# Output projections with the last two head blocks held back and four outputs begun early, in a hybrid attention encoder on one Trainium2 core

## The chip, the core and the metric

The kernel runs on one core of a Trainium2 chip. The metric is device time in microseconds (us). Five engines work in parallel, each through its own queue in order: PE (matrix products), DVE (VectorE, elementwise), ACT (ScalarE, activations and copies), POOL (GpSimd, elementwise) and SP (which issues the transfers). They meet only in semaphores.

## The reference

512 tokens of width 1024 go through two residual mixer layers, each followed by a SwiGLU feed-forward block, in float32. Layer 0 mixes by latent attention and dilated windows, layer 1 by grouped-query attention. What matters here is the end of each mixer and the start of its feed-forward block:

```python
x = x + heads @ w_out                      # heads: 6 (layer 0) or 8 (layer 1) blocks of 128 columns
n = x * rsqrt(mean(x * x) + 1e-6) * gain   # RMS norm over the 1024 columns
f = silu(n @ w_gate) * (n @ w_up)          # hidden width 2816 = 22 blocks of 128
x = x + f @ w_down
```

## The kernel before

Everything is held transposed: x is eight tiles d8 to d15 of 128 columns by 512 tokens. A float32 number is split into a high part (float32r) and a remainder, and a product is three matmuls (lines L165 to L167: high by high, high by low, low by high). A weight load (`load`) is a transfer, a high copy on ACT (L154) and a subtraction on POOL (L155). A scheduler fixes each engine's order when the program is built, so what the source writes is not always the order on the engine.

**Mixer's end.** `mix_part` projects the head blocks that are ready early, one output tile after the other, and adds each to x (L645, DVE); its matmuls fill the gaps between the attention's steps. The last block comes from the last attention head: its weighted sum (pv) goes through ACT and DVE (L363, L366, L368) before PE may use it. `mix_last` then projects the late blocks for all eight outputs n, one after the other, each in a PSUM bank of the tag `acc`, of which there are two. After the add (L655) `nr.feed` makes the next layer's input parts of tile n: high on ACT (L207), low on DVE (L208, reads two SBUF tiles), and a square on ACT (L198), summed on POOL (L202).

**Start of the feed-forward block.** Gate and up products (`og`, `ou`) of hidden blocks f0 and f1 start from those parts before the norm is known. The norm's column sums are eight one-column matmuls (L220), then DVE (L223), POOL's power (L225), and four matmuls that spread it (L232). The products of f1 beyond the first three blocks are written behind the spread. After it DVE makes the scaled inputs (L692, L693) and their sums for a seven-product scheme (`sums`: L671 to L683; the last low parts of each pair are L683) and the results of f0 to f3 (L863 to L866). In `Seven` a unit adds weight tiles into the sums `tab` and `bias` and splits each into high (ACT, L180) and low (DVE, L181). The products named b11, b21, t1 to t4, b22 are matmuls of 256 columns (L742).

Of the kernel before, what the change touches and what calls it, by code (L numbers as in the profile page):

```python
# [9 lines left out]
F32 = mybir.dt.float32  # L10
F32R = mybir.dt.float32r
AF = mybir.ActivationFunctionType
ALU = mybir.AluOpType
AX = mybir.AxisListType

P = 128
# [9 lines left out]
FIRST = 4  # L26
# [5 lines left out]
QTAGS = ("pt", "pt", "acc")  # L32
WARM = 14
HP, NHP = 100, 200
QFIRST = 3
GOUT = {6: (0, 3), 12: (3, 6)}
FILL = [1] * 12 + [2] * 4
# [56 lines left out]
def encoder_kernel(ctx: ExitStack, tc: tile.TileContext, a, out):  # L94
    nc = tc.nc
# [7 lines left out]
    def psum(tag):  # L103
        return ps.tile([P, 512], F32, tag=tag, bufs=BANKS[tag], name=f"ps_{tag}")
# [5 lines left out]
    def E(dt=F32):  # L110
        return U("e", dt, bufs=4)
# [32 lines left out]
    def load(views, k, low=None):  # L144
        raw = U("wraw", bufs=2, shape=(P, WCOLS))
        hi = U("whi", F32R, bufs=3, shape=(P, WCOLS))
        lo = U("wlo", F32R, bufs=3, shape=(P, WCOLS))
        n = 0
        for v in views:
            a, b = v.shape[1], v.shape[2]  # L150
            nc.sync.dma_start(raw[:, n:n + a * b].rearrange("p (a b) -> p a b", a=a), v)
            n += a * b
        r, h, l = raw[:, :n], hi[:, :n], lo[:, :n]
        nc.scalar.copy(h, r)  # L154
        (low or nc.gpsimd).tensor_sub(l, r, h.bitcast(F32))  # L155
        if k is None:
            return h, l
        return h.rearrange("p (k n) -> p k n", k=k), l.rearrange("p (k n) -> p k n", k=k)

    def wview(w, k0, k1, n0, n1):  # L160
        return w[k0 * P:k1 * P, n0:n1].rearrange("(k p) n -> p k n", p=P)

    def mm3(dst, lhs, rhs, first, last):

        nc.tensor.matmul(dst, lhsT=lhs[0], rhs=rhs[0], start=first, stop=False)  # L165
        nc.tensor.matmul(dst, lhsT=lhs[0], rhs=rhs[1], start=False, stop=False)  # L166
        nc.tensor.matmul(dst, lhsT=lhs[1], rhs=rhs[0], start=False, stop=last)  # L167
# [15 lines left out]
    class Norm:  # L183


        def __init__(self, dst=None):
            self.dst = dst
            self.parts = []
            self.acc = U("nacc", bufs=2)
            self.sums = [self.acc]  # L190
            self.n = 0
# [83 lines left out]
    for k in range(KB):  # L275
# [4 lines left out]
        xt = E()  # L280
# [126 lines left out]
    for k in range(3):  # L407
        o = proj(wblock(k * P), xs, QTAGS[k])
# [29 lines left out]
    hd0 = Heads([(f"d{b}", f"d{4 + b}") for b in range(4)] + [("d16", "d17"), ("d18", "d19")])  # L438


    for sp in range(2):
# [9 lines left out]
        o = block(0, 0)  # L451
# [4 lines left out]
        o = block(1, 0)  # L456
# [5 lines left out]
        for g in (1, 2):  # L462
            o = block(0, g)
            qf[g] = U(f"d{5 + g}")
            nc.vector.scalar_tensor_tensor(qf[g], o, 0.125, rbc, op0=ALU.mult, op1=ALU.mult)
            o = block(1, g)
            kf[g] = U(f"d{7 + g}")
            nc.vector.tensor_mul(kf[g], o, rbc)
        for g in range(3):
            o = block(2, g)  # L470
# [162 lines left out]
    def mix_part(xt, wo, heads, part):  # L633
        ks = [k for k0, k1 in part for k in range(k0, k1)]
        def get(n):
            return load([wview(wo, k0, k1, n * P, (n + 1) * P) for k0, k1 in part], len(ks)) if n < KB else None
        w = get(0)
        for n in range(KB):
            nw = get(n + 1)
            o = psum("acc")  # L640
            for i, k in enumerate(ks):
                mm3(o, (w[0][:, i, :], w[1][:, i, :]), heads.parts[k], i == 0, i == len(ks) - 1)
                if i < len(ks) - 1:
                    yield 0
            nc.vector.tensor_add(xt[n], xt[n], o)  # L645
            w = nw
            yield 0

    def mix_last(xt, wo, heads, ks, nr, g):
        ws = [load([wview(wo, k, k + 1, 0, DM)], 1) for k in ks]  # L650
        for n in range(KB):
            o = psum("acc")
            for i, k in enumerate(ks):
                mm3(o, [t[:, 0, n * P:(n + 1) * P] for t in ws[i]], heads.parts[k], i == 0, i == len(ks) - 1)
            add = nc.vector.tensor_add(xt[n], xt[n], o)  # L655
            if n:
                with tc.issue_after(add.ins):
                    nr.feed(xt[n - 1], gain(g, n - 1))
        nr.feed(xt[KB - 1], gain(g, KB - 1))
# [8 lines left out]
    def sums(cb, ya, yb, temps, b11, b2, t12_to, t34_to):  # L668

        t12, t34 = temps  # L670
        nc.vector.tensor_sub(t12[:, 0:H], ya[:, H:T], ya[:, 0:H])  # L671
        nc.vector.tensor_sub(t12[:, H:T], yb[:, H:T], t12[:, 0:H])
        nc.vector.tensor_sub(t34[:, 0:H], ya[:, 0:H], t12[:, H:T])
        nc.vector.tensor_sub(t34[:, H:T], yb[:, 0:H], t12[:, H:T])
        split(*b11, ya[:, 0:H])
        cb["b11"].append(b11)
        h, l = b2
        split(h, l, yb)
        cb["b21"].append((h[:, 0:H], l[:, 0:H]))
        cb["b22"].append((h[:, H:T], l[:, H:T]))  # L680
        for j, (src, (h, l)) in enumerate(((t12, t12_to), (t34, t34_to))):
            nc.scalar.activation(h, src, AF.Copy, scale=-1.0)
            nc.vector.scalar_tensor_tensor(l, src, -1.0, h.bitcast(F32), op0=ALU.mult, op1=ALU.subtract)  # L683
            for q in range(2):
                cb[f"t{2 * j + q + 1}"].append((h[:, q * H:q * H + H], l[:, q * H:q * H + H]))

# [15 lines left out]
    class Seven:  # L702

        count = 0

        def __init__(self, loads, cb):
            self.cb = cb
            par = Seven.count % 2
            Seven.count += 1
            self.w = w = len(cb["b11"]) * P  # L710
            rg = U("wraw", bufs=2, shape=(P, WCOLS))[:, 0:2 * w]
            u1, u2 = (U(f"m{4 + 2 * par + j}")[:, 0:w] for j in range(2))
            at = {"g": rg, "g1": rg[:, 0:w], "g2": rg[:, w:], "u1": u1, "u2": u2}
            for name, v in loads:
                nc.sync.dma_start(at[name].rearrange("p (k n) -> p k n", n=P), v)
            g1, g2 = at["g1"], at["g2"]
            sab = U("tab", shape=(P, 2, T)).rearrange("p a b -> p (a b)")[:, 0:2 * w]
            sdc = U("bias", shape=(P, 9 * P))[:, 0:2 * w]
            self.g = self.parts(rg)
            nc.vector.tensor_add(sab[:, 0:w], u1, u2)  # L720
            nc.vector.tensor_add(sab[:, w:], sab[:, 0:w], g1)
            self.a = self.parts(sab)
            nc.vector.tensor_add(sdc[:, 0:w], sab[:, w:], g2)
            nc.vector.tensor_add(sdc[:, w:], u1, g1)
            self.d = self.parts(sdc)
            uh, ul = U("oT", F32R, bufs=2)[:, 0:w], U(("m12", "otmp")[par], F32R)[:, 0:w]
            nc.scalar.copy(uh, u2)  # L727
            nc.gpsimd.tensor_sub(ul, u2, uh.bitcast(F32))  # L728
            self.u = uh, ul
# [6 lines left out]
        def product(self, o, w, half, name, first):  # L736
            n = len(self.cb[name])
            for i in range(n):
                c = slice(half * self.w + i * P, half * self.w + (i + 1) * P)
                x = self.cb[name][i]  # L740
                for j, (wt, xp) in enumerate(((w[0], x[0]), (w[0], x[1]), (w[1], x[0]))):
                    nc.tensor.matmul(o[:, 0:H], lhsT=wt[:, c], rhs=xp, start=first and i == 0 and j == 0,  # L742
                                     stop=i == n - 1 and j == 2, skip_group_check=True)
# [29 lines left out]
    def ffn(xt, nr, layer, tail=None):  # L773
# [36 lines left out]
        def hidden(f):  # L810
            v = [("g", wview(w1, 0, KB, f * P, (f + 1) * P))]
            v += [(f"u{h + 1}", wview(w1, 4 * h, 4 * h + 4, FF + f * P, FF + (f + 1) * P)) for h in range(2)]
            gg = U(f"m{8 + f % 2}")

            def second(o, e):
                nc.vector.tensor_add(gg[:, 0:H], o, e[:, 0:H])

            def third(o, e):
                nc.vector.tensor_add(gg[:, H:T], o, e[:, H:T])
                nc.scalar.activation(gg, gg, AF.Silu)  # L820

            def seventh(o, e):
                raw[f] = U(f"m{10 + f % 2}")
                nc.vector.tensor_add(raw[f][:, H:T], o, e[:, T:T + H])

            def fourth(o, e):
                nc.vector.tensor_mul(raw[f][:, 0:H], o, gg[:, 0:H])
                nc.vector.tensor_mul(raw[f][:, H:T], raw[f][:, H:T], gg[:, H:T])

            return Seven(v, cb).run(second, third, seventh, fourth)  # L830

        def output(f0, f1, j):
            x1, x2 = xt[2 * j], xt[2 * j + 1]
# [21 lines left out]
        for f in range(FIRST):  # L855
# [12 lines left out]
            if f == 0:  # L868
                cb = combine(xt, nr.spread_ps, ("ffn_norm", layer))
# [6 lines left out]
        order = []  # L876
# [38 lines left out]
    xt = [U(f"d{8 + n}") for n in range(KB)]  # L915
# [3 lines left out]
        bx = [B(i) for i in range(4)]  # L919
        return Norm([(bx[k // 4][:, k % 4, :], bx[2 + k // 4][:, k % 4, :]) for k in range(KB)])  # L920

    for _ in mix_part(xt, a["w_out_ab"][0], hd0, ((0, 3), (4, 6))):
        pass
    nr = split_inputs()
    mix_last(xt, a["w_out_ab"][0], hd0, (3,), nr, ("ffn_norm", 0))
    for n, sub in ffn(xt, nr, 0):
        if n == 0:
            norm = Norm(X())
# [39 lines left out]
    for c in range(NT):  # L968
# [4 lines left out]
                                       op0=ALU.mult, op1=ALU.subtract)  # L973
# [109 lines left out]
    nr = split_inputs()  # L1083
# [75 lines left out]
```

## Time and profile before

| | |
|---|---|
| median of 3 runs | 1238.76 us (1237.95 to 1240.36) |
| the profiled execution's own time | 1239.44 us |
| its span | 1237.5 us |
| busy time, PE / DVE / ACT / POOL | 1213.4 / 954.2 / 681.8 / 464.4 us |

The span is what the profile covers, from first to last instruction; the run's own time is 1.94 us longer. The table's busy times overlap; shares over the whole span are averages over stages that differ much. Times in rows count from the span's start.

### The profile page before, as it was taken

To read this page: it belongs to the slowest core of one execution; us is meant where nothing else is said; L and a number is where in the kernel's file an instruction comes from. 1 tells how busy PE (TensorE), PEld (TensorE's weight loads), DVE (VectorE), ACT (ScalarE), POOL (GpSimd) and SP (SyncE) were. 2 spreads that over 40 slices of the span, in tenths; PEclk is the share of its full clock that TensorE was granted. 3 is DMA by queue.
4 is the path that set the end of the run, shared out by engine and by line. 5 is a ranking of instruction groups with operands and counts; after the bars stand their busy time and mean duration, and the time that the engine had idled before them with its cause. 6 is when DMAs were issued, how large, how long until landed. Compare 5 with 4: busy or idle time off the path is not lost.

```text
span 1237.5 us, 20871 instructions
## 1 busy us (share of the span) xinstructions
PE 1213.4 (98%) x7757; PEld 1075.9 (87%) x7757; DVE 954.2 (77%) x1729; ACT 681.8 (55%) x1221; POOL 464.4 (38%) x347
## 2 busy tenths in 40 slices
PE   8999999999999999999999999999999999999997
PEld 7887788777778999999998877787788999999996
DVE  4543437983894999999965778988596799999984
ACT  5424437783653565456545477777454556456554
POOL 5544334444624022111224487756633122111210
PEclk9999999999999999999999999999999999999999
DMA  9343323213214333333324332113222333343331
GB/s 288 91 102 88 92 58 89 79 58 99 80 55 120 111 103 103 107 107 97 110 76 130 98 96 48 39 34 97 75 88 86 111 103 103 104 116 100 101 111 69
DMA packets 204725, 118.20 MB, mean 96 GB/s; under 512 B 17186, under 2 KB 196432, under 8 KB 204624
## 3 DMA queue, kind: packets, MB, share of 16 engines
q1 hardware_dynamic: 202848, 113.70, 32.4%
q10 hardware_dynamic: 1776, 3.17, 0.7%
q8 instruction: 61, 1.00, 0.3%
q14 instruction: 40, 0.33, 0.1%
HBM read 106.09 MB, written 4.19 MB: 89 GB/s over the span
## 4 chain that ended last, share of the span: by engine, by line
PE 84%; DVE 9%; DMA 3%; POOL 2%; ACT 1%; issue 1%; SPq 0%; POOLq 0%; DVEq 0%; ACTq 0%
PE ps_s L742 23%; PE ps_pt L742 11%; PE ps_acc L165 8%; PE ps_acc L166 8%; PE ps_acc L167 8%; PE ps_acc L742 6%; PE ps_pt L347 3%; PE ps_s L167 2%; PE ps_s L166 2%; PE ps_s L165 2%; PE ps_o L375 1%; PE ps_o L374 1%; DVE b L181 1%; PE ps_pt L165 1%; PE ps_pt L166 1%
## 5 line engine op out<-in xcount | busy, mean ns | idle before, releaser
L155 POOL TENSOR_TENSOR wlo<-wraw,whi 128x1024 fp32r<-128x1024 f32 (+3 forms) x99 | 185.1, 1872 | 176.3 <-ACT whi L154 166.2
L154 ACT CAST whi<-wraw 128x1024 fp32r<-128x1024 f32 (+3 forms) x106 | 87.8, 832 | 133.9 <-PE ps_acc L166 64.4
L728 POOL TENSOR_TENSOR m<-m,oT 128x512 fp32r<-128x512 f32 (+1 forms) x26 | 48.8, 1875 | 245.2 <-ACT oT L727 245.2
L165 PE MATMUL ps_acc<-x,whi 128*128 128x512 f32 x280 | 111.6, 401 | 1.8 <-DVE x L366 0.8
L167 PE MATMUL ps_acc<-x,wlo 128*128 128x512 f32 x280 | 112.1, 400 | 0.0
L166 PE MATMUL ps_acc<-x,whi 128*128 128x512 f32 x280 | 112.0, 400 | 0.0
L742 PE MATMUL ps_s<-x,whi 128*128 128x256 f32 x576 | 106.4, 282 | 0.0
L728 POOL TENSOR_TENSOR otmp<-m,oT 128x512 fp32r<-128x512 f32 (+1 forms) x26 | 42.5, 1634 | 153.3 <-ACT oT L727 149.4
L181 DVE TENSOR_TENSOR b<-ps_pt,b 128x512 fp32r<-128x512 f32 x112 | 75.0, 682 | 18.9 <-ACT b L180 18.7
L742 PEld LDWEIGHTS ps_s<-x,whi 128*128 128x128 f32 x576 | 88.8, 188 | 0.4
L180 ACT CAST whi<-bias 128x1024 fp32r<-128x1024 f32 (+1 forms) x52 | 52.8, 1016 | 58.5 <-PE ps_s L742 27.7
L742 PE MATMUL ps_s<-x,wlo 128*128 128x256 f32 x288 | 81.1, 281 | 0.0
L180 ACT CAST b<-ps_pt 128x512 fp32r<-128x512 f32 x112 | 63.7, 584 | 28.1 <-PE ps_pt L347 27.3
L180 ACT CAST whi<-tab 128x1024 fp32r<-128x1024 f32 (+1 forms) x52 | 53.0, 1019 | 45.5 <-PE ps_s L742 38.1
L165 PEld LDWEIGHTS ps_acc<-x,whi 128*128 128x128 f32 x280 | 52.5, 189 | 13.9 <-issue 1.2
L181 DVE TENSOR_TENSOR wlo<-bias,whi 128x1024 fp32r<-128x1024 f32 (+1 forms) x52 | 61.2, 1177 | 3.9 <-ACT whi L180 3.0
L181 DVE TENSOR_TENSOR wlo<-tab,whi 128x1024 fp32r<-128x1024 f32 (+1 forms) x52 | 62.6, 1204 | 1.8 <-ACT whi L180 1.8
L181 DVE TENSOR_TENSOR wlo<-wraw,whi 128x1024 fp32r<-128x1024 f32 (+1 forms) x52 | 63.1, 1213 | 0.7 <-ACT whi L180 0.7
L166 PEld LDWEIGHTS ps_acc<-x,whi 128*128 128x128 f32 x280 | 52.7, 188 | 12.3 <-POOL x L368 0.5
L180 ACT CAST whi<-wraw 128x1024 fp32r<-128x1024 f32 (+1 forms) x52 | 52.7, 1014 | 19.1 <-PE ps_acc L166 6.4
L167 PEld LDWEIGHTS ps_acc<-x,wlo 128*128 128x128 f32 x280 | 52.8, 189 | 11.3
L742 PE MATMUL ps_pt<-x,whi 128*128 128x256 f32 x288 | 54.3, 282 | 1.8 <-DVE x L683 1.8
(495 smaller groups left out, 4012.0 us busy)
## 6 DMA issues: line engine op xcount, KB each, us to landing
wraw<-in_ffn_w_in_dram SPq DMA_DIRECT2D x52, 512.0 KB, 3.9
m<-in_ffn_w_in_dram SPq DMA_DIRECT2D x72, 256.0 KB, 3.1
wraw<-in_w_in_ab_dram SPq DMA_DIRECT2D x21, 512.0 KB, 3.7
wraw<-in_ffn_w_out_dram SPq DMA_DIRECT2D x40, 256.0 KB, 3.0
m<-in_ffn_w_out_dram SPq DMA_DIRECT2D x16, 256.0 KB, 3.5
wraw<-in_gqa_w_q_dram SPq DMA_DIRECT2D x8, 512.0 KB, 4.1
m<-in_ffn_w_out_dram SPq DMA_DIRECT2D x16, 192.0 KB, 3.0
wraw<-in_ffn_w_out_dram SPq DMA_DIRECT2D x16, 192.0 KB, 2.9
```

The source lines that it names most:

```text
L154: nc.scalar.copy(h, r)
L155: (low or nc.gpsimd).tensor_sub(l, r, h.bitcast(F32))
L165: nc.tensor.matmul(dst, lhsT=lhs[0], rhs=rhs[0], start=first, stop=False)
L166: nc.tensor.matmul(dst, lhsT=lhs[0], rhs=rhs[1], start=False, stop=False)
L167: nc.tensor.matmul(dst, lhsT=lhs[1], rhs=rhs[0], start=False, stop=last)
L180: nc.scalar.copy(hi, src)
L181: nc.vector.tensor_sub(lo, src, hi.bitcast(F32))
L347: nc.tensor.transpose(pt[:, k * P:(k + 1) * P], p[:, k * P:(k + 1) * P], ident)
L374: nc.tensor.matmul(o, lhsT=vs[k][:, h, :], rhs=pth[:, k, :], start=k == 0, stop=False)
L375: nc.tensor.matmul(o, lhsT=vs[k][:, h, :], rhs=ptl[:, k, :], start=False, stop=k == NT - 1)
L728: nc.gpsimd.tensor_sub(ul, u2, uh.bitcast(F32))
L742: nc.tensor.matmul(o[:, 0:H], lhsT=wt[:, c], rhs=xp, start=first and i == 0 and j == 0, stop=i == n - 1 and j == 2, skip_group_check=True)
```

## The change

Three edits. `mix_last` begins the first late block's product for four outputs before the others, in the banks acc, acc, s, s, and lets the further outputs rotate over these four banks. In layer 0 head block 2 moves from `mix_part` to `mix_last` (24 matmuls): eight weight loads become 512 instead of 640 columns wide, and there is one more load of 1024 columns. In the first unit of each feed-forward block the split of the sum `bias` is issued only after the low part of the last t12 (L683, after: L690).

```diff
+LEAD = ("acc", "acc", "s", "s")
...
     def mix_last(xt, wo, heads, ks, nr, g):
         ws = [load([wview(wo, k, k + 1, 0, DM)], 1) for k in ks]
+        def product(o, n, i):
+            mm3(o, [t[:, 0, n * P:(n + 1) * P] for t in ws[i]], heads.parts[ks[i]], i == 0, i == len(ks) - 1)
+
+        begun = [psum(tag) for tag in LEAD]
+        for n, o in enumerate(begun):
+            product(o, n, 0)
         for n in range(KB):
-            o = psum("acc")
-            for i, k in enumerate(ks):
-                mm3(o, [t[:, 0, n * P:(n + 1) * P] for t in ws[i]], heads.parts[k], i == 0, i == len(ks) - 1)
+            o = begun[n] if n < len(begun) else psum(LEAD[n % len(LEAD)])
+            for i in range(1 if n < len(begun) else 0, len(ks)):
+                product(o, n, i)
             add = nc.vector.tensor_add(xt[n], xt[n], o)
...
-            nc.vector.scalar_tensor_tensor(l, src, -1.0, h.bitcast(F32), op0=ALU.mult, op1=ALU.subtract)
+            low = nc.vector.scalar_tensor_tensor(l, src, -1.0, h.bitcast(F32), op0=ALU.mult, op1=ALU.subtract)
+            if j == 0:
+                cb["last"] = low.ins
...
-        def __init__(self, loads, cb):
+        def __init__(self, loads, cb, early=False):
+
+            order = tc.issue_after(cb["last"]) if early else nullcontext()
             self.cb = cb
...
-            self.d = self.parts(sdc)
+            with order:
+                self.d = self.parts(sdc)
...
-            return Seven(v, cb).run(second, third, seventh, fourth)
+            return Seven(v, cb, f == FIRST).run(second, third, seventh, fourth)
...
-    for _ in mix_part(xt, a["w_out_ab"][0], hd0, ((0, 3), (4, 6))):
+    for _ in mix_part(xt, a["w_out_ab"][0], hd0, ((0, 2), (4, 6))):
         pass
     nr = split_inputs()
-    mix_last(xt, a["w_out_ab"][0], hd0, (3,), nr, ("ffn_norm", 0))
+    mix_last(xt, a["w_out_ab"][0], hd0, (2, 3), nr, ("ffn_norm", 0))
```

The scheduler answers to this with other orders at places that the diff does not name. On PE in layer 0, before, the last of the norm's column sums (L220) and the spread (L232) stand apart; `ps_pt` is f1's gate, `ps_s` f0's two products:

```order
1243 L220 MATMUL ps_o<-ones,nacc 128x1
1244 L220 MATMUL ps_o<-ones,e 128x1
1245 L166 MATMUL ps_s<-b_2942,whi 128x512
1246 L167 MATMUL ps_s<-b_2940,wlo 128x512
1247 L166 MATMUL ps_s<-b_2942,whi 128x512
1248 L167 MATMUL ps_s<-b_2940,wlo 128x512
1249 L167 MATMUL ps_pt<-b_2939,wlo 128x512
...
1255 L167 MATMUL ps_pt<-b_2939,wlo 128x512
1256 L232 MATMUL ps_o<-ident,rcol 128x128 x4
```

The same place after the change (lines are one higher there):

```order
1255 L167 MATMUL ps_pt<-b_2917,whi 128x512
1256 L168 MATMUL ps_pt<-b_2915,wlo 128x512
1257 L221 MATMUL ps_o<-ones,nacc 128x1
...
1264 L221 MATMUL ps_o<-ones,e 128x1
1265 L233 MATMUL ps_o<-ident,rcol 128x128 x4
1266 L166 MATMUL ps_pt<-b_2915,whi 128x512
1267 L167 MATMUL ps_pt<-b_2917,whi 128x512
```

Eleven matmuls that stood between column sums and spread now stand ahead of the sums; the spread follows them directly. In layer 1 it is the same (29 matmuls stood between before, none now).

POOL in layer 0 before, from the projection's weights (640 wide) to the power:

```order
79 L155 TENSOR_TENSOR wlo<-wraw,whi 128x640 x5
80 L155 TENSOR_TENSOR wlo<-wraw,whi 128x1024 x3
81 L202 TENSOR_TENSOR nacc<-nacc,e 128x512 x6
82 L155 TENSOR_TENSOR wlo<-wraw,whi 128x1024
83 L225 TENSOR_TENSOR rcol<-tiny,mhalf 128x4
84 L155 TENSOR_TENSOR wlo<-wraw,whi 128x1024 x5
```

And after:

```order
82 L156 TENSOR_TENSOR wlo<-wraw,whi 128x512
83 L156 TENSOR_TENSOR wlo<-wraw,whi 128x1024 x3
84 L203 TENSOR_TENSOR nacc<-nacc,e 128x512 x3
85 L156 TENSOR_TENSOR wlo<-wraw,whi 128x1024
86 L203 TENSOR_TENSOR nacc<-nacc,e 128x512
87 L156 TENSOR_TENSOR wlo<-wraw,whi 128x1024
88 L203 TENSOR_TENSOR nacc<-nacc,e 128x512 x2
89 L156 TENSOR_TENSOR wlo<-wraw,whi 128x1024 x2
90 L226 TENSOR_TENSOR rcol<-tiny,mhalf 128x4
91 L156 TENSOR_TENSOR wlo<-wraw,whi 128x1024 x3
```

Weights of f0, f1 and f2 now stand between the sums of squares and ahead of the power: four from the first sum on, where there was one. In layer 1 six sums, two weights and the power stood in a row; now it is four sums, a weight, a sum, a weight, a sum, two weights and the power.

DVE in layer 0 before alternates adds and low parts:

```order
331 L655 TENSOR_TENSOR d_2731<-d_2731,ps_acc 128x512
332 L655 TENSOR_TENSOR d_2732<-d_2732,ps_acc 128x512
333 L208 SCALAR_TENSOR_TENSOR b_2941<-d_2731,gcol,b_2939 128x512
334 L655 TENSOR_TENSOR d_2733<-d_2733,ps_acc 128x512
335 L208 SCALAR_TENSOR_TENSOR b_2941<-d_2732,gcol,b_2939 128x512
336 L655 TENSOR_TENSOR d_2734<-d_2734,ps_acc 128x512
337 L208 SCALAR_TENSOR_TENSOR b_2941<-d_2733,gcol,b_2939 128x512
```

And after, outputs 4 to 7, the end of the stretch:

```order
338 L209 SCALAR_TENSOR_TENSOR b_2917<-d_2734,gcol,b_2915 128x512
339 L209 SCALAR_TENSOR_TENSOR b_2917<-d_2732,gcol,b_2915 128x512
340 L662 TENSOR_TENSOR d_2737<-d_2737,ps_s 128x512
341 L662 TENSOR_TENSOR d_2738<-d_2738,ps_s 128x512
342 L662 TENSOR_TENSOR d_2736<-d_2736,ps_acc 128x512
343 L209 SCALAR_TENSOR_TENSOR b_2918<-d_2735,gcol,b_2916 128x512
344 L209 SCALAR_TENSOR_TENSOR b_2918<-d_2737,gcol,b_2916 128x512
345 L209 SCALAR_TENSOR_TENSOR b_2918<-d_2738,gcol,b_2916 128x512
346 L209 SCALAR_TENSOR_TENSOR b_2918<-d_2736,gcol,b_2916 128x512
```

The adds stand earlier, and four low parts follow one another at the end.

## Rows read from the trace of the kernel before

**Rows 1.** the page's head: span, and busy time with share and instructions by engine.

```profile
span 1237.5 us, 20871 instructions
...
PE 1213.4 (98%) x7757; PEld 1075.9 (87%) x7757; DVE 954.2 (77%) x1729; ACT 681.8 (55%) x1221; POOL 464.4 (38%) x347
```

**Rows 2.** PE's waits, 250:304, 304:333, 333:372, 865:893; us, times, longest.

```profile
PE ps_s L165 <- DVE p L337: 0.7, 2, 0.5
PE ps_o L374 <- DVE oT L363: 0.4, 1, 0.4
PE ps_pt L347 <- DVE b L181: 0.3, 1, 0.3
...
PE ps_s L166 <- DVE b L208: 1.0, 1, 1.0
...
PE ps_pt L742 <- DVE x L683: 1.8, 1, 1.8
...
PE ps_acc L165 <- DVE x L366: 0.8, 1, 0.8
PE ps_acc L165 <- DVE d L655: 0.3, 1, 0.3
```

**Rows 3.** DVE in order of time (start us, us, engine, line), 307 to 332.

```profile
307.95 0.69 DVE L655 TENSOR_TENSOR d<-d,ps_acc 128x512 f32<-128x512 f32 x1
...
309.62 2.37 DVE L208 SCALAR_TENSOR_TENSOR b<-d,gcol,b 128x512 fp32r<-128x512 f32 x1
...
312.51 1.18 DVE L208 SCALAR_TENSOR_TENSOR b<-d,gcol,b 128x512 fp32r<-128x512 f32 x1
```

**Rows 4.** POOL in order of time, the same stretch.

```profile
309.04 2.40 POOL L155 TENSOR_TENSOR wlo<-wraw,whi 128x1024 fp32r<-128x1024 f32 x1 [1.93 <-PE ps_acc L167]
311.40 1.74 POOL L202 TENSOR_TENSOR nacc<-nacc,e 128x512 f32<-128x512 f32 x1
...
327.29 1.02 POOL L225 TENSOR_TENSOR rcol<-tiny,mhalf 128x4 f32<-128x4 f32 x1 [1.44 <-DVE tiny L223]
```

**Rows 5.** DVE in order of time, the same stretch of layer 1.

```profile
872.78 0.75 DVE L208 SCALAR_TENSOR_TENSOR b<-d,gcol,b 128x512 fp32r<-128x512 f32 x1 [0.20 <-ACT b L207]
```

**Rows 6.** ACT in order of time, layer 0.

```profile
327.38 1.05 ACT L154 CAST whi<-wraw 128x1024 fp32r<-128x1024 f32 x1 [3.69 <-PE ps_s L166]
```

**Rows 7.** PE in order of time, L220 to L232, layer 0.

```profile
324.70 0.28 PE L220 MATMUL ps_o<-ones,nacc 128*128 128x1 f32 x2
...
326.64 0.36 PE L220 MATMUL ps_o<-ones,e 128*128 128x1 f32 x2
...
329.28 0.40 PE L167 MATMUL ps_pt<-b,wlo 128*128 128x512 f32 x1
329.51 1.05 PE L232 MATMUL ps_o<-ident,rcol 128*128 128x128 f32 x8
```

**Rows 8.** PE in order of time, the same in layer 1.

```profile
891.53 0.63 PE L166 MATMUL ps_s<-b,whi 128*128 128x512 f32 x1
891.96 0.58 PE L167 MATMUL ps_s<-b,wlo 128*128 128x512 f32 x1
...
897.04 1.05 PE L232 MATMUL ps_o<-ident,rcol 128*128 128x128 f32 x8
```

**Rows 9.** busy us (and instructions) of PE, PEld, DVE, ACT, POOL; PEclk.

```profile
885.00:890.00 5.00, 4.91 (x28) 4.02 (x27) 3.04 (x3) 1.67 (x3) 5.00 (x3) 0.90 0.18 51
890.00:895.00 5.00, 5.00 (x19) 3.92 (x18) 0.00 (x0) 1.05 (x1) 3.81 (x3) 0.76 0.55 162
...
365.00:370.00 5.00, 2.94 (x22) 2.53 (x22) 4.18 (x7) 2.62 (x6) 1.30 (x1) 1.00 0.00 0
```

**Rows 10.** DVE in order of time, last sums of the inputs, layer 0.

```profile
364.29 0.68 DVE L720 TENSOR_TENSOR tab<-m,m 128x512 f32<-128x512 f32 x1
364.89 0.68 DVE L865 TENSOR_TENSOR m<-ps_acc,rbc 128x512 f32<-128x512 f32 x1
...
366.16 1.21 DVE L181 TENSOR_TENSOR wlo<-bias,whi 128x1024 fp32r<-128x1024 f32 x1
```

## Prediction, made before the run

> **What bounds the kernel now.** Read the page's head first [rows 1]: PE is busy 1213.4 of 1237.5 us, so the whole program holds at most 24 us of PE idleness, and a change that adds no arithmetic moves the time only by PE's waits or by its clock. Then ask what PE waited for in the stretches that the change touches [rows 2]. In layer 0 the attention's tail (250 to 304 us) shows waits of 0.7, 0.4 and 0.3 us behind DVE's softmax work; the output projection's end (304 to 333) shows 1.0 us, behind a low part of the next inputs (L208); the start of the feed-forward block 1.8 us, behind the last low part of t12 (L683). In layer 1 it waits 0.8 us for the last head (L366) and 0.3 us for an add that frees a bank (L655). The third view is the clock by stretches [rows 9]: 0.90 and 0.76 of full speed from 885 to 895, where layer 1's column sums end, and 1.00 elsewhere in these stretches, even across the 1.8 us wait. Levels are 2.4 and 1.2 GHz; at the lower one two neighbouring 512-column matmuls start 0.43 us apart [rows 8], at the higher one 0.23 [rows 7]. The loss in those ten microseconds is 5 x 0.10 + 5 x 0.24 = 1.7 us. All that the change can aim at is about 1.4 + 1.0 + 1.8 + 0.3 + 1.7 = 6 us, half a per cent; 0.2%, about 2.5 us, is what measurement can tell from no change.
>
> **The change part by part.** The number of matmuls is the same; I give only waits and clock, layer by layer, minus for time saved. The weight columns also stay equal (8 x 640 + 1024 before, 8 x 512 + 2 x 1024 after), so POOL and ACT do the same work in another order.
>
> *Layer 0, attention tail.* The scheduler now puts 29 more projection matmuls (6.7 us of PE at 0.23) ahead of the last pv. That can fill all of the 1.4 us [rows 2], or, since the order of DVE's steps there changes too, cost as much as one of those waits. I take -1.0, between -1.4 and +0.5.
>
> *Layer 0, the eight outputs.* The 1.0 us behind L208 goes [rows 2]: the first four adds come early, from partial sums begun before the last head. What is late next are the low parts of outputs 4 to 7. Look at L208 beside POOL. With POOL idle it takes 0.75 us [rows 5]. Against a weight's subtraction on POOL from 309.04 to 311.44 it takes 2.37 and ends at 311.99, 0.55 after POOL; against the sum of squares ending at 313.14 it ends at 313.69, again 0.55 after [rows 3, 4]. That sum of squares, which began while L208 ran, itself took 1.74 us and ended 1.15 after L208. The add L655, with one input in PSUM, takes 0.69 us in a stretch with POOL busy [rows 3]. So each of the two holds the other up. I replay the new order with these prices, t = 0 at the first product of the last head block. Outputs are complete at 1.4, 1.8, 2.3, 3.7, 5.1, 6.5, 7.9 and 9.3 us (pitch 0.23); f0's gate starts at 9.1 and needs the low parts of outputs 4, 6, 7, 5 at 12.6, 17.0, 17.7 and 18.4. The first four are done at 9.5. The next starts at 11.2 and meets f0's second weight on POOL (10.6 to 13.0; its high copy on ACT, 1.05 us [rows 6], is ready by then): it ends at 13.55, 1.0 late. Taking turns with a sum of squares (1.15 after), a weight (2.25 after) and another sum, the others end at 15.3, 18.1 and 19.8; the last is another 0.4 late. Together +1.4. Without any hold-up all four would be ready before they are needed, 0; with every meeting at its longest the replay gives 3.75.
>
> The Trainium skill, "SBUF — State Buffer", section "Who interferes with whom", says that a DVE instruction with two SBUF inputs and a GpSimd instruction that reads SBUF exclude one another, whoever comes first holding the port for its whole instruction. The rows above agree (0.55 us behind each end). It speaks against this change: by it the stretch costs the +1.4, without it 0.
>
> *Layer 0, the spread.* Before, eleven matmuls lay between the column sums and L232, and PE went from one to the other without a gap [rows 7]; they covered DVE's L223 and POOL's 1.02 us power, which began at 327.29, 0.3 after the last column sum ended at 327.00 [rows 4, 7]. Now they stand ahead, so PE has nothing until the power is done: 1.3 us plus a passing of 0.1 = 1.4. POOL's two weights ahead of the power must be done too; f2's ends in the replay about when the column sums do (24 + 2.2 against 23.7 + 2.4 on POOL), so it may add up to one more us. I take +1.4, between 0.7 and 2.4. Queued behind the spread in PE's order is the rest of f1, and behind it on DVE everything that is scaled.
>
> *Layer 0, t1.* Ahead of the last low part of t12 stood L720 and the two adds and splits behind it: 0.6 us each for the first two (the step from 364.29 to 364.89) and 1.2 for the split [rows 10]. They are now behind it, so it ends 2.4 us earlier after the spread. PE now asks for it some 1.4 us sooner, since its t1 products stand together (an estimate: twelve matmuls of 256 columns at half the 0.23), so 1.0 of the 1.8 us wait goes, and the split of `bias` follows at once and is what b22 waits for. -1.0, between -1.8 and 0.
>
> *Layer 0, clock and output.* Column sums of one column (324.70 to 327.00) and the wait behind them are over 3.5 us with hardly any column in PE. In layer 1 the clock was low just behind the column sums [rows 8, 9]. If it falls here, most of the 1.7 us is hidden, since PE waits for DVE later in this stretch anyway; +0.4, between 0 and 1.7.
>
> Layer 0: -1.0 - 1.0 + 1.4 + 1.4 - 1.0 + 0.4 = +0.2.
>
> *Layer 1, what goes.* The bank wait of 0.3 and the 1.7 us of low clock that now lie between the column sums and L232, -2.0 (from -2.2 to -0.3, if the clock falls again in the same place). The 0.8 us for the last head stays: POOL, ACT and DVE take as long for it.
>
> *Layer 1, the eight outputs.* The same replay with this layer's order, where low parts come in the order 0 to 7, and f0's gate from 8.4 on needs number 4 at 11.4 and 5 at 12.6: number 4 ends at 11.9 behind four sums of squares, number 5 at 14.75 behind a weight, 2.25 late together. In the trace low parts of this layer ran shorter than in layer 0 where POOL was idle (0.75 [rows 5]), so I take +1.9, between 0 and 3.75.
>
> *Layer 1, the spread.* 29 matmuls of cover have gone, and the replay has f2's weight end 0.5 after the column sums: +1.6, between 0.7 and 2.4.
>
> *Layer 1, t1 and clock.* The add L865 now stands ahead of the last t12 (0.6 [rows 10]); of that 0.4 shows. A low clock behind the spread finds less slack than in layer 0, since PE is nearly the bound there: +0.4, between 0 and 1.7.
>
> Layer 1: -2.0 + 1.9 + 1.6 + 0.4 + 0.4 = +2.3. Both: +2.5. The profiled execution's own time 1239.44 becomes 1241.9; it lies 0.7 above the median of the three runs, so against that median the forecast is 1238.76 + 2.5 = 1241.2 us, on the edge of what can be told from no change.
>
> The rules of the clock: the Trainium skill, "TensorE: Matmul & The Clock Gate", Part 1, calls the half clock the default state and says that activity releases it. The trace agrees where it fell behind layer 1's column sums (0.76 of full speed), and by the page both layers would lose 1.7 us behind the new wait.
>
> **Rivals.**
> *Slower, the clock falls in both layers and shows.* The place is the stretch from the first column sum to some microseconds behind the spread; the price is 1.7 per layer in place of 0.4, +2.6, so 1243.8. It decides if f1 and f2 after the spread end later than DVE's t12. For it: rows 8 and 9. Against: the 1.8 us wait at 366 left the clock at 1.00 [rows 9].
>
> *Faster, POOL gives way.* If the L202s and weights on POOL start in the gaps of DVE, low parts take 0.75 us [rows 5], the feeds run ahead of PE, and with them the 1.4 and 1.9 go: 1237.9; then PE reaches the column sums without an earlier wait, the clock stays up (-0.8), and the tail's wait goes wholly (-0.4), t1's too (-0.8): 1235.9. For it: the adds now come from four banks, early. Against: both low parts shown of layer 0 met POOL [rows 3, 4].
>
> *Nothing moves.* Waits that go in one place come back before the next wait of the same chain; the sum stays within 1 us: 1238.8. For it: all waits here are of the size of one instruction.
>
> **How the numbers follow.** Forecast 0.42 (its own range 1239.3 to 1243.2, half of it over the 2.5 us border), slower rival 0.17, faster rival 0.27, nothing moves 0.14. Faster by over 0.2%: 0.26 (the faster rival nearly whole). Slower: 0.20 + 0.17 = 0.37. Within: the rest, 0.37. The range that leaves out no more than 2 in 10 goes from a faster rival somewhat over its price, 1235.4, to the slower rival and a little of the long ends, 1244.6.
>
> **What would show it.** In the changed profile: no PE wait behind L208's first low part but one or two behind outputs 4 to 7 (new L209), of 1 to 2 us; a PE wait behind POOL's power of 1.3 to 2 us in each layer directly ahead of the spread; the low clock behind it; t12's last low part followed at once by the split of `bias`, and a PE wait there of under a microsecond. The prediction is wrong if the power's wait is hidden, if low parts on DVE end at 0.75 us each, or if the tail of layer 0 loses its cover.

## The result, and the profile after

The change made the kernel slower: 1248.8 us (median of 6 runs, 1247.24 to 1250.37) against 1239.71 for the kernel before (6 runs), a ratio of 1.0082, 95% interval 1.0071 to 1.0092. The medians differ by 9.1 us, and the interval is 8.8 to 11.4 us; 2.5 had been forecast, with 1244.6 as the top of the range. The profiled span grew from 1237.5 to 1246.9 us.

The first view is what PE waited for in the profile after, by stretches: the eight outputs and the spread of layer 0, its t1 and b22 products, and the outputs and the spread of layer 1 (us, times, longest). It answers to [rows 2].

```profile
PE ps_o L233 <- POOL rcol L226: 1.5, 1, 1.5
PE ps_s L167 <- DVE b L209: 1.4, 1, 1.4
PE ps_s L166 <- DVE d L662: 0.8, 1, 0.8
...
PE ps_pt L754 <- DVE x L690: 1.3, 1, 1.3
PE ps_pt L754 <- DVE wlo L182: 0.8, 1, 0.8
PE ps_s L754 <- ACT p L762: 0.4, 1, 0.4
...
PE ps_s L166 <- DVE d L662: 2.2, 1, 2.2
PE ps_acc L166 <- DVE x L367: 0.5, 1, 0.5
...
PE ps_o L233 <- POOL rcol L226: 1.9, 1, 1.9
```

The reader is to see three kinds. The power before the spread (L226) and a low part (L209) were forecast, at 1.4, 1.6 and 1.4 us. A wait for an add (L662) ahead of a matmul into an `s` bank was not: f0's gate writes to `s`, and the bank was still held by a late output. Nothing is left of the 1.4 us in the attention's tail: no row answers to it from 250 to 300.

The second view is the clock by stretches after, to be read with [rows 9]; the column behind POOL's is the granted share of full speed. The last line is the stretch that begins with layer 1's spread.

```profile
330.00:335.00 5.00, 4.99 (x19) 4.35 (x20) 2.30 (x4) 2.83 (x4) 0.00 (x0) 0.66 0.36 105
370.00:375.00 5.00, 4.93 (x27) 4.86 (x28) 3.58 (x5) 2.22 (x6) 2.58 (x3) 0.66 0.18 52
885.00:890.00 5.00, 3.38 (x8) 2.73 (x9) 5.00 (x5) 4.38 (x7) 4.92 (x4) 0.66 0.00 0
905.00:910.00 5.00, 4.75 (x25) 4.02 (x26) 2.94 (x5) 3.16 (x5) 0.19 (x1) 1.00 0.38 109
```

Between 250 and 960 us the clock before was low once (0.90 and 0.76, 1.7 us lost); now it is low three times, each 5 x 0.34 = 1.7 us: behind the spread's wait, behind the waits at t1 of layer 0, and behind the wait for the bank in layer 1. Behind the 1.9 us wait at layer 1's spread it stayed at 1.00. The third view is PE in order of time where it falls first, answering to [rows 7].

```profile
330.01 2.04 PE L233 MATMUL ps_o<-ident,rcol 128*128 128x128 f32 x8 [1.50 <-POOL rcol L226]
331.70 0.77 PE L166 MATMUL ps_pt<-b,whi 128*128 128x512 f32 x1
332.27 0.63 PE L167 MATMUL ps_pt<-b,whi 128*128 128x512 f32 x1
```

The spread begins at 330.01, 0.5 later than before, which is near the forecast for this place (-1.0 - 1.0 + 1.4 + 1.4 = +0.8). But it now takes 2.04 us in place of 1.05, and all of DVE's work that follows waits for it, by way of a copy on ACT. Low parts and adds on DVE in layer 0, and POOL beside them:

```profile
310.82 1.27 DVE L662 TENSOR_TENSOR d<-d,ps_s 128x512 f32<-128x512 f32 x2
312.02 0.67 DVE L662 TENSOR_TENSOR d<-d,ps_acc 128x512 f32<-128x512 f32 x1
312.62 8.53 DVE L209 SCALAR_TENSOR_TENSOR b<-d,gcol,b 128x512 fp32r<-128x512 f32 x4
```

```profile
312.00 2.41 POOL L156 TENSOR_TENSOR wlo<-wraw,whi 128x1024 fp32r<-128x1024 f32 x1
314.36 1.75 POOL L203 TENSOR_TENSOR nacc<-nacc,e 128x512 f32<-128x512 f32 x1
316.07 2.85 POOL L156 TENSOR_TENSOR wlo<-wraw,whi 128x1024 fp32r<-128x1024 f32 x1
```

Four low parts in a row take 8.53 us, 2.1 each, in turns with two weights and the sums; the prediction's replay had from 11.2 to 19.8, 8.6 us. The adds of outputs 6 and 7, which free the `s` banks, stand at 310.82, behind four low parts.

### The profile page after: what moved, and what is told of

It reads as the page before. It is cut to its first block, busy times and chain, and to the rows that moved or that the text cites. A ratio compares the mean times of both kernels' runs of the same rounds, so it can differ in the third digit from the quotient of the medians.

```text
span 1246.9 us, 20864 instructions
## 1 busy us (share of the span) xinstructions
PE 1216.4 (98%) x7757; PEld 1079.4 (87%) x7757; DVE 960.8 (77%) x1729; ACT 680.7 (55%) x1222; POOL 464.9 (37%) x348
## 4 chain that ended last, share of the span: by engine, by line
PE 82%; DVE 11%; DMA 2%; POOL 2%; ACT 2%; issue 1%; SPq 0%; POOLq 0%; DVEq 0%; ACTq 0%
PE ps_s L754 22%; PE ps_pt L754 11%; PE ps_acc L167 8%; PE ps_acc L166 8%; PE ps_acc L168 8%; PE ps_acc L754 6%; PE ps_pt L348 3%; PE ps_s L166 2%; PE ps_s L168 2%; PE ps_s L167 2%; DVE b L209 1%; PE ps_o L376 1%; PE ps_o L375 1%; POOL wlo L156 1%; PE ps_s L500 1%
## 5 line engine op out<-in xcount | busy, mean ns | idle before, releaser
L155 ACT CAST whi<-wraw 128x1024 fp32r<-128x1024 f32 (+3 forms) x107 | 88.1, 826 | 128.1 <-PE ps_acc L167 56.6
L166 PE MATMUL ps_acc<-x,whi 128*128 128x512 f32 x272 | 108.3, 400 | 1.3 <-ACT e L1042 0.7
L168 PE MATMUL ps_acc<-x,wlo 128*128 128x512 f32 x272 | 109.0, 401 | 0.0
L167 PE MATMUL ps_acc<-x,whi 128*128 128x512 f32 x272 | 108.7, 400 | 0.0
L166 PEld LDWEIGHTS ps_acc<-x,whi 128*128 128x128 f32 x272 | 51.1, 189 | 12.6 <-ACT e L1042 1.2
L167 PEld LDWEIGHTS ps_acc<-x,whi 128*128 128x128 f32 x272 | 51.2, 188 | 11.7 <-POOL x L369 0.5
```

## The experiments

The ratio is to the kernel before, run beside each on the same chip. Its median there was 1239.71 us for the changed kernel, 1240.69 for a1 to a4, 1239.62 for b1 to b4 and 1241.09 for c1 to c4, so two runs are compared by the last column, the difference of the medians to the kernel before.

| run | median us | ratio to before (95%) | us to before |
|---|---|---|---|
| changed kernel | 1248.8 | 1.0082 (1.0071 to 1.0092) | +9.1 |
| a1, without early outputs | 1234.7 | 0.9953 (0.9941 to 0.9966) | -6.0 |
| a2, early outputs alone | 1257.5 | 1.0140 (1.0126 to 1.0154) | +16.8 |
| a3, later outputs in acc | 1243.9 | 1.0033 (1.0020 to 1.0046) | +3.2 |
| a4, nine matmuls as cover | 1246.3 | 1.0044 (1.0030 to 1.0058) | +5.6 |
| b1, late split alone | 1238.1 | 0.9991 (0.9982 to 1.0000) | -1.5 |
| b2, banks acc, acc, pt, pt | 1258.2 | 1.0153 (1.0139 to 1.0166) | +18.5 |
| b3, a3 and a4 together | 1245.1 | 1.0043 (1.0030 to 1.0055) | +5.5 |
| b4, a1 with sums on DVE | 1248.3 | 1.0070 (1.0057 to 1.0084) | +8.7 |
| c1, adds and low parts by turns | 1246.4 | 1.0040 (1.0026 to 1.0054) | +5.4 |
| c2, c1 with later outputs in acc | 1239.8 | 0.9994 (0.9982 to 1.0006) | -1.3 |
| c3, a1 with three blocks held, layer 0 | 1240.6 | 0.9994 (0.9984 to 1.0003) | -0.5 |
| c4, a1 with three blocks held, layer 1 | 1240.2 | 0.9991 (0.9982 to 1.0000) | -0.9 |

**Which edit it is.** a1 takes the first edit back:

```diff
-        begun = [psum(tag) for tag in LEAD]
-        for n, o in enumerate(begun):
-            product(o, n, 0)
         for n in range(KB):
-            o = begun[n] if n < len(begun) else psum(LEAD[n % len(LEAD)])
-            for i in range(1 if n < len(begun) else 0, len(ks)):
+            o = psum("acc")
+            for i in range(len(ks)):
                 product(o, n, i)
```

> The change without its first edit: block 2 is still held back in layer 0 and the bias split still issued late, but the eight outputs are projected one after the other in the two acc banks. Theory A (the loss comes from the four outputs begun early in acc, acc, s, s, which lengthens waits for banks, low parts and the spread): the time goes back to between 1236 and 1241 us, no wait of PE for an add in an s bank, none for the power. Rival B (holding block 2 back and splitting bias late cost most of it): 1244 us or more.

Measured: 1234.7 us, faster than before by 0.47% (6.0 us) and than the changed kernel by 15 us. That is below theory A's range and far from rival B's. No wait of PE is listed from 300 to 345. Column sums and spread stand apart again (29 matmuls between them in both layers):

```profile
318.49 0.36 PE L221 MATMUL ps_o<-ones,e 128*128 128x1 f32 x2
...
327.10 1.05 PE L233 MATMUL ps_o<-ident,rcol 128*128 128x128 f32 x8
```

In this kernel the third edit changes nothing: without it every engine has the same order, since the scheduler puts the split there anyway. So a1 against before is what holding block 2 back is worth: 6 us. In the two traces it is 4.7 us, and not all of that lies where block 2 is: by PE's place (the time at which the same number of matmuls is behind it) a1 is 2.0 us ahead at the attention's tail and 3.4 at 400 us; 2.0 more come in layer 1, where all engines have the order of before, but the clock stayed at 1.00 from 885 to 895. How often that fall comes in either kernel is not shown. In layer 0 the clock falls behind the column sums in a1 (0.89 from 315 to 320, 0.77 from 320 to 325), and costs 1.7 us there; with a lower time all the same.

a2 is the opposite, the first edit alone (`hd0, (3,), nr` and the blocks of `mix_part` as before, no late split).

> The first edit alone: four outputs begun early and the rotation over acc, acc, s, s, but block 2 projected as before and the bias split as before. Theory A: 1245 to 1250 us, with PE waits of 1.5 to 2 us for the power in both layers and 2 us for an add in an s bank in layer 1. Rival B: 1238 to 1242 us.

Measured: 1257.5 us. With one late block in layer 0 every early product already needs the last head. Its waits, layer 0:

```profile
PE ps_o L233 <- POOL rcol L226: 3.1, 1, 3.1
PE ps_s L754 <- ACT p L762: 1.6, 1, 1.6
PE ps_pt L754 <- DVE wlo L182: 1.1, 1, 1.1
```

Layer 1 has the 2.2 us for an add in an `s` bank and 1.9 for the power that theory A asks for, so its direction and its waits hold; its range (up to 1250) is missed by 7 us. The first edit alone (+16.8) and block 2 alone (-6.0) add up to 10.8, and the change measured 9.1. b1 is the third edit alone.

> The third edit alone: bias split behind the last t12, nothing else of the change. Against before only DVE's order differs. From the trace of before: the last low part of t12 in layer 0 comes 1.2 to 2.4 us earlier and the 1.8 us wait of PE for it shrinks; b22's weights then wait for the split. Theory (the edit helps a little): 1237 to 1239.5 us, with before at 1240. Rival (the order only turns the wait into one for the split): within 1 us of before.

Measured: 0.9991, within the bound of what can be told from no change, so neither expectation is decided. The order differs from before only in layer 0, at one place on DVE and one on ACT. PE's wait there for the last low part of t12 went from 1.8 to 0.7 us.

**Why early outputs cost.** a3 and a4 each cure one wait of the changed kernel. a3:

```diff
-            o = begun[n] if n < len(begun) else psum(LEAD[n % len(LEAD)])
+            o = begun[n] if n < len(begun) else psum("acc")
```

> The changed kernel, but from the fifth output on the outputs take acc banks, so that an s bank is given back after outputs 2 and 3 and f0's gate does not have to wait for outputs 6 and 7. Seven matmuls stand between the norm's column sums and the spread. If the bank wait (0.8 us in layer 0, 2.2 in layer 1) and the low clock behind it matter: 4 to 6 us less than the changed kernel, 1243 to 1245. If the low parts set the pace in any case, so that PE waits for them instead: within 2 us of the changed kernel.

Measured: 1243.9, 5.9 us less, as the first expectation had it. No wait for an add in `s` is left; in layer 1 others take part of its place:

```profile
PE ps_s L167 <- DVE b L209: 2.3, 3, 1.4
PE ps_o L233 <- POOL rcol L226: 2.0, 1, 2.0
```

a4 puts work between column sums and spread (`last_sum` is the last matmul of the column sums; f1's gate begins behind it with its first three blocks):

```diff
-            og = proj(load([wview(w1, 0, KB, f * P, (f + 1) * P)], KB), xs, tags[0], after, 3)
+            og = proj(load([wview(w1, 0, KB, f * P, (f + 1) * P)], KB), xs, tags[0], after, 3,
+                      nr.last_sum if f == 1 else None)
```

> The changed kernel, but the first nine matmuls of f1's gate are issued after the norm's column sums, so that they lie between these and the spread and PE has 2.1 us of work while DVE and POOL make the reciprocal root. If the spread without cover is the loss: its waits of 1.5 and 1.9 us go, the clock does not fall in layer 0 at 330 us, and the time falls by 4 to 7 us to 1242 to 1245. If what follows is set by DVE alone, counted from the power: within 1.5 us of the changed kernel, the waits only move ahead of the column sums or behind the spread.

Measured: 1246.3, 3.5 us less, somewhat under the 4 to 7 expected. In layer 0 the wait for the power shrank from 1.5 to 0.9 and the clock stayed up; in layer 1 it stayed at 1.8, since POOL's two weights ahead of the power ended only at 901.2, 3 us after the last column sum. b3 has both cures.

> Both cures together: outputs from the fifth on in acc and nine matmuls of f1 behind the column sums. If bank wait and spread add up: below both single cures, 1238 to 1242 us. If the low parts of outputs 4 to 7 are the common cause behind both: no better than the better of the two, 1243 to 1246, with PE waits for low parts of 2 us and more in layer 1.

Measured: 1245.1, 3.6 us less, so they don't add up, as the second expectation had it; what stays is PE waiting for low parts, in layer 1:

```profile
PE ps_s L167 <- DVE b L210: 3.0, 4, 1.4
```

b2 moves the early outputs to other banks, `LEAD = ("acc", "acc", "pt", "pt")`.

> The changed kernel with the four outputs in banks acc, acc, pt, pt. f0's gate, in s, then needs no bank of the outputs, so its waits for an add (0.8 and 2.2 us) must go; f1's products, in pt, need them later. If the s banks are what the early outputs cost: 1241 to 1244 us. If it is the spread without cover and the low parts next to one another, which this leaves as they are: 1245 to 1249 us.

Measured: 1258.2, worse than both expectations. No wait for an add is left in layer 0, but waits for low parts of 5.4 us:

```profile
PE ps_s L167 <- DVE b L209: 5.4, 3, 3.5
PE ps_o L233 <- POOL rcol L226: 1.4, 1, 1.4
```

So the `s` bank is one place where the delay shows and not all of it: when it is not the bank, PE meets the low parts a little later. Why b2 is 9 us worse than the changed kernel was not taken apart.

c1 keeps the early outputs and their banks, but makes DVE take adds and low parts by turns:

```diff
-            add = nc.vector.tensor_add(xt[n], xt[n], o)
+            with tc.issue_after(nr.low) if n > 1 else nullcontext():
+                add = nc.vector.tensor_add(xt[n], xt[n], o)
```

> The changed kernel with its four outputs begun early, but each add from the third on is issued after the low part of the output two before, so that DVE alternates adds and low parts as before the change; four banks as in the change. The scheduler then puts 15 and 4 matmuls between column sums and spread again and one or two weights less before the power. Theory C (the loss is the run of adds that early outputs allow: it pushes low parts behind one another and, through the scheduler, weights ahead of sums and matmuls ahead of the column sums): 1234 to 1240 us. Rival (the early products or the s banks themselves cost it): 1244 us or more.

Measured: 1246.4, 3.7 us less. The theory's number fails and the rival's holds: with four banks rotating the adds that free `s` now stand later, and PE waits for them, directly (layer 1, second group) or through the high part of a late output (layer 0, first group):

```profile
PE ps_s L166 <- ACT b L208: 2.9, 1, 2.9
...
PE ps_s L166 <- DVE d L663: 2.4, 1, 2.4
```

c2 has this order and gives the later outputs acc banks.

> As the kernel with alternating adds, and outputs from the fifth on take acc banks, which puts 30 matmuls between column sums and spread. Theory C: 1233 to 1237 us, like the kernel without early outputs, and no wait of PE for an add in an s bank. Rival: as c1.

Measured: 1239.8, between theory C's range and the rival's c1, better than c1 by 6.6 us and than a3 by 4.5. So both count: of 15 us between the changed kernel and a1, the order of adds alone gives 3.7, the banks alone 5.9, both 10.4. Part of this is the clock: in c1's trace it is low from 310 to 320 (0.76, 0.55), from 885 to 890 (0.66) and from 900 to 910 (0.82, 0.50), 8.5 us lost, in c2's only from 320 to 325 (0.67), 1.7 lost; waits and clock are not separated here. The other 4.7 us between c2 and a1 stay open. By PE's place in the two traces, 5.3 us apart, 1.3 of them arise in the first 17 us of the kernel, which no edit touches (clock 0.77 from 5 to 20 us, in a1 0.89), 1.4 between 303 and 321, 1.6 in layer 1 between the column sums and t1, and the rest in smaller pieces.

**Do low parts and POOL hold one another up?** b4 takes a1 and gives the six sums of squares (L203) to DVE; on PE one matmul moves in each layer, on ACT one instruction.

```diff
-                    nc.gpsimd.tensor_add(self.acc, self.acc, sq)
+                    self.adder.tensor_add(self.acc, self.acc, sq)   # nc.vector for these two norms
```

> The kernel without early outputs (1234.7 us), in which the six sums of squares of each feed-forward norm go from POOL to DVE; PE's order stays. Theory (DVE and POOL hold one another up whenever both read two tiles in SBUF): the eight low parts, 13.6 us together with POOL's sums beside them, take 0.75 us each but for those beside a weight, 7 to 10 us together, and the six sums cost DVE 0.6 to 0.7 each. Rival (low parts are slow for another reason, for instance PSUM adds before them): they keep their 1.2 to 1.7 us each and the stretch becomes 4 us longer.

Groups on DVE over layer 0's outputs (count, busy us, mean ns): first a1, then b4, whose lines are one higher; last, b4's end of the stretch in order of time, DVE and then POOL.

```profile
L209 DVE SCALAR_TENSOR_TENSOR b<-d,gcol,b 128x512 fp32r<-128x512 f32 x8 | 10.3, 1287 | 0.6 <-ACT b L208 0.6
```

```profile
L210 DVE SCALAR_TENSOR_TENSOR b<-d,gcol,b 128x512 fp32r<-128x512 f32 x8 | 8.0, 1006 | 0.0
L204 DVE TENSOR_TENSOR nacc<-nacc,e 128x512 f32<-128x512 f32 x6 | 6.3, 1044 | 0.0
```

```profile
315.44 0.74 DVE L210 SCALAR_TENSOR_TENSOR b<-d,gcol,b 128x512 fp32r<-128x512 f32 x1
316.11 2.85 DVE L204 TENSOR_TENSOR nacc<-nacc,e 128x512 f32<-128x512 f32 x1
318.88 2.85 DVE L210 SCALAR_TENSOR_TENSOR b<-d,gcol,b 128x512 fp32r<-128x512 f32 x1
```

```profile
315.72 5.46 POOL L156 TENSOR_TENSOR wlo<-wraw,whi 128x1024 fp32r<-128x1024 f32 x2 [11.73 <-ACT whi L155]
```

Seven of the eight low parts took 0.74 us, and the last, beside a weight on POOL, 2.85; of the sums five took 0.68 and one, beside the other weight, 2.85. The hold-up is shown. It is seen as longer instructions and not as a wait for a semaphore, so the chip's section, in which the engines meet only in semaphores, leaves it out. As a kernel it is 14.7 us worse than a1: PE waits 2.0 us in each layer for the last sum, and the clock falls behind it. Note that a1, whose time was the base of this expectation, had 10.3 and not 13.6 us.

**More of what helped.** c3 holds blocks 1, 2 and 3 of layer 0.

> Without early outputs, and blocks 1, 2 and 3 of layer 0 are projected at the end instead of 2 and 3. If what holding back gives is cover for the last low parts and for the head's way through ACT and DVE, which a second block covers already: within 2 us of 1234.7. If low parts of the eight outputs still set the pace, 24 more matmuls between them give another 1 to 2 us: 1232.5 to 1234. A third weight in three buffers may hold f0's weights back: up to 1239.

Measured: 1240.6, 5.5 us worse than a1 and above all three expectations. PE now waits 2.0 us for the last head's way through DVE (L367), of which a1 shows nothing, and the clock falls behind it (0.66 from 300 to 305). The third expectation comes nearest: PE also waits 1.1 us for the high copy of a weight (L155) ahead of f0's gate, but what the weight buffers alone cost was not measured. c4 holds three blocks in layer 1.

> Without early outputs, blocks 2 and 3 held in layer 0, and in layer 1 three head blocks (5 to 7) projected at the end instead of two. PE's wait of 0.8 us there for the last head should go and the outputs come 0.7 us further apart, as in layer 0: 1232 to 1234.5 us. If the attention's gaps miss the filling: 1236 or more.

Measured: 1240.2, 5.1 us worse than a1; the second expectation holds. At the attention's end PE waits 2.0 us for ACT's copies and the wait for the last head grew from 0.8 to 1.9:

```profile
PE ps_o L375 <- ACT b L181: 2.0, 2, 1.2
PE ps_acc L166 <- DVE x L367: 1.9, 1, 1.9
```

The best version is a1, 1234.7 us, faster than both kernels.

## Why the prediction was wrong, point by point

*Direction.* The forecast lay on the edge between no change and slower, with 0.37 on slower; the loss was 9.1 us where 2.5 had been forecast. The slower rival (the clock falls in both layers and shows) is the nearest, and its 1243.8 too low; behind the spread the clock fell in layer 0 alone. None of the three signs named for being wrong appeared (a hidden wait for the power, low parts of 0.75 us each, a tail without cover). What failed is the size of the clock, the sign of t1 and a wait left out. PE's place, after against before, shows where (minus is ahead):

| stretch | forecast | traces |
|---|---|---|
| layer 0, attention's tail, to 303 us | -1.0 | -2.0 |
| layer 0, outputs, spread and clock, to 335 | +2.2 | +4.2 |
| layer 0, t1, to 400 | -1.0 | +1.8 |
| from there to layer 1's last head, 840 | 0 | +0.7 |
| layer 1, to 950 | +2.3 | +4.8 |

*Attention tail, -1.0.* Right in direction, and larger than the range allowed (-1.4): the listed waits of 1.4 us are gone and PE is 2.0 ahead. That the spread began near its forecast time is in part luck, since this gain and the waits behind it were both larger than forecast.

*Low parts, +1.4 and +1.9.* In layer 0 the replay of DVE and POOL was right (8.53 us for 8.6), but the 1.4 came as one wait, for the last low part, and not as 1.0 and 0.4; PE had already lost 0.8 for an `s` bank, so the equal sum is luck. In layer 1 the queue of low parts was there, but PE met it earlier, at f0's first matmul, as 2.2 us for an `s` bank whose add stands behind low parts. The order shows that f0's gate and the last outputs use the same tag; only the low parts were priced. This step, "the eight outputs", left a wait out. Two readings in it are off without moving the sum: layer 1's two numbers, 0.5 and 1.65 late, give 2.15 and not 2.25, and the add shown in [rows 3] at 307.95 lay where POOL was idle (an add of 0.68 us at 311.91, beside the sum of squares from 311.40, bears the reading out).

*The spread, +1.4 and +1.6.* Right: 1.5 and 1.9.

*The clock, +0.4 and +0.4, and layer 1's -1.7.* This term was mis-sized most. I let it hide behind PE's later wait for DVE. But the spread itself ran at the low clock and took 1.0 us longer, ahead of DVE's whole chain: PE's place went from 0.5 to 2.2 us behind while the clock was low and stayed at 2.2 to 365, so nothing of this 1.7 was hidden. A second fall came behind the waits at t1, where waits and clock together are 2.4 us more than before and PE's place moved by 1.8. In layer 1 no fall came behind the spread; the low clock that was to go (-1.7) came back at 885, behind the bank wait. Three stretches of 1.7 us in place of one make 3.4 us, where 0.8 - 1.7 = -0.9 had been counted: 4.3 us of the 6.6, less the 0.6 hidden at t1. The -1.7 also rested on one execution: a1 and b1 have layer 1's order of before, and their clock was 1.00 from 885 to 895. The profiled execution of the changed kernel is not a special one: the mean granted clock of its six was 0.991 to 0.994, that of the five of a1 0.996 to 0.997.

*t1, -1.0 and +0.4.* Failed in layer 0. The last low part of t12 did move ahead of `tab`, `bias` and the add, but it came only 0.3 us sooner, counted from DVE's first instruction behind the spread (368.41 - 332.70 = 35.7 after, 367.29 - 331.28 = 36.0 before). The gain was taken by meetings with POOL's weights, which now fell on dearer places. Before, three meetings on this way cost DVE some 3.8 us; the two dearest:

```profile
336.33 2.28 DVE L671 TENSOR_TENSOR oT<-p 128x256 f32<-128x256 f32 x1
...
349.19 2.29 DVE L721 TENSOR_TENSOR tab<-tab,wraw 128x512 f32<-128x512 f32 x1
```

After, one of 1.6 us at 339 and two more, 5.8 together. DVE after, and POOL:

```profile
344.17 2.78 DVE L690 SCALAR_TENSOR_TENSOR x<-rbc,x 128x512 fp32r<-128x512 f32 x1
...
352.27 2.79 DVE L182 TENSOR_TENSOR m<-m,m 128x512 fp32r<-128x512 f32 x1
```

```profile
344.00 2.39 POOL L156 TENSOR_TENSOR wlo<-wraw,whi 128x1024 fp32r<-128x1024 f32 x1 [3.24 <-ACT whi L155]
352.11 2.40 POOL L156 TENSOR_TENSOR wlo<-wraw,whi 128x1024 fp32r<-128x1024 f32 x1 [5.71 <-ACT whi L155]
```

Both begin 0.16 to 0.17 us behind a weight and wait it out, 2.1 us each above the 0.68 that such an instruction takes undisturbed [rows 10]. That is where I had priced a moved instruction by its own duration and not by whom it meets. The wait for this low part was 1.3 us and not under one, with 0.8 and 0.4 beside it. In layer 1 PE waited 0.7 us for it, where 0.4 had been forecast and nothing was listed before.

*The faster rival.* POOL did not give way; b4 shows the hold-up and its absence.

*What I did not see at all:* the edits taken apart have opposite signs. Holding block 2 back is worth -6 us, the early outputs +15 on top of it. My terms were sums over the whole change, and the early outputs' order was taken as given with the rest.

## What to carry to other kernels

Beginning several accumulations early gained nothing here, where the engine that empties them was the one in demand: it made that engine do the cheap adds first and the work that PE waits for last, and it held banks that the next product needs. Price a change's edits one by one, since a scheduler answers to each with a new order, and look in that order for who holds the bank that the next matmul writes. A wait of 1.5 us cost twice that (1.5 and 1.7) where the clock fell behind it and the matmuls that then ran slowly were the ones for which another engine waited. Whether it falls is not settled by the order alone, so look at more than one execution before a fall is counted as a gain or a loss.

## What the runs showed of the hardware that was not expected

The spread's matmuls (float32, 128 x 128; four in the program, eight in the profile) took 2.04 us at the low clock and 1.05 at the high one. In the changed kernel the clock fell behind a wait of 1.5 us with one-column matmuls ahead of it (330) and behind one of 2.2 us (886.6), and not behind the 1.9 us at layer 1's spread, which also had one-column matmuls ahead (1.00 from 905 to 910), nor behind the 1.83 us at 366 in the kernel before. Of the six spreads that had no matmul between column sums and spread (both layers of the changed kernel, a2 and b2) that one alone had no fall beside it (a2: 0.66 from 335 to 340, 0.50 from 910 to 915; b2: 0.70 from 335 to 340, 0.50 from 905 to 910). What decides it was not found.

Two DVE instructions of 0.68 us, each begun 0.16 to 0.17 us behind a weight's subtraction on POOL, took 2.78 and 2.79 us and ended 0.56 us after it.
